# A hybrid block on one core: the queries and forget gates of heads 0 and 1 become a fourteenth seven-product unit, and their recurrence runs in the index stage

## The chip, the core and the metric

The kernel runs on one core of one Trainium2 chip. The core has a matrix engine (TensorE, PE in the profile, its weight loads PEld), a vector engine (VectorE, DVE), an activation engine (ScalarE, ACT), GpSimd (POOL) and SyncE (SP), which in this kernel issues nearly all transfers. Each engine works through its own instructions in order and waits on semaphores for the others. The metric is the device time of one execution in microseconds; the lower the better. The time before is 1340.77 us, the median of 3 runs (1340.67 to 1341.74).

## What is computed

One layer over 512 tokens of 2048 features, all in float32. The normalised input is projected by `w_in`; two branches follow, are each projected back to 2048 features, weighed by sigmoid gates, summed, projected once more, added to the input and normalised. The reference, cut to what matters:

```python
proj = rmsnorm(x, norm_w) @ w_in
a_q, a_f, a_i, a_g, c_q, c_kv, k_idx_raw, w_idx_raw, b_g, m_a, m_b = split(proj)
# branch A: gated linear recurrence, 8 heads of 128, chunks of 64 tokens
q = silu(a_q) * 128 ** -0.5
f = lb + (1 - lb) * sigmoid(a_f); k = 1 - f; log_f = log(f); v = a_i
y_a = rmsnorm(recurrence(q, k, log_f, v), gnorm_w) * silu(a_g)
# branch B: an indexer with 16 heads scores all keys, the best 128 a query are kept
score = sum_h relu(q_idx @ k_idx.T) * w_idx
y_b = softmax(q @ k_sel.T * 128 ** -0.5 + t5_bias) @ v_sel * silu(b_g)   # 8 heads of 128
merged = sigmoid(m_a) * (y_a @ w_pa) + sigmoid(m_b) * (y_b @ w_pb)
out = rmsnorm(x + merged @ w_out, final_norm_w)
```

The recurrence multiplies a state by the forget gate at each token, adds key times value, and reads it with the query.

## The kernel before

**Matmuls.** A float32 product is made of three matmuls on halves that carry a high and a low part (`mm3`, lines 74 to 77). The halves of the weights are made on the way: ScalarE writes `wh` (L71), VectorE subtracts to get `wl` (L72), from a raw tile `wr` that SP has loaded (L128). Two raw tiles exist; `load_ahead` keeps at most two loads beyond the splits, and `prep(i, ahead=3)` emits the splits up to two steps beyond the one in hand.

**Jobs.** The program is a list of jobs, emitted one after the other, which is also the order on every engine. `feat_job` projects `ntile` tiles of 128 features over `nk` blocks of the contraction, `kc` blocks to a step, with 512 tokens as columns. `pair_unit` computes 512 features at once by a scheme of seven products in place of eight: matrices are cut in quarters, VectorE and ScalarE make sums of quarters of the weights (`pair_sums`, L145 to L154), and each of 8 steps runs 7 products x 2 tiles x 3 matmuls of 256 columns. The gates of both branches go through eleven such units (`gate_pair`), and the queries and forget gates of head pairs 2 and 3 through two more (`pair_job` with `pair_evac` into `qf_d` in DRAM). Pairs 0 and 1 are projected by `af_aq(p)`: two `feat_job`s with two tiles and 16 blocks each.

**Lanes.** Work that isn't a large projection is written as generators in lanes (`hgrn` the recurrences, `top` the selection of keys, `att` attention, `norm`, `misc`, `t5`). `pump()` loads ahead, runs postponed stores (`flush`: a store asked for in `late` goes out two pumps later) and then takes one step of the first generator of each lane. `feat_job` pumps after each tile of a step when it has fewer than four tiles, else after each second one; with `often` also after block 1 of each tile. `drain(name)` runs a lane to its end at once.

**Recurrence** (`hgrn_gen(p)`, heads 2p and 2p+1). Seven levels: at odd levels TensorE computes scores into a bank `hl` (L80), VectorE multiplies by the decay (L784) and takes the scores over (L791, L797); at even levels ScalarE first copies (`keep`, L807), then VectorE multiplies again. Then keys are transposed (`hkt`), states (`hp`, `hst`) and outputs (`ho`) computed, normalised (`hz`), gated and stored to `ya_d` (L917). `R.load` tells the selection (`top_gen`) how much VectorE time a step takes; a round of the selection (two instructions over a block of scores, 48 rounds) is emitted when its credit, 2.7 less `R.load` at each pump, is above zero.

**Banks.** Eight PSUM banks: four `acc` for projections, four `sd`, handed out in turn, for the lanes and the indexer. An index head takes three `sd` banks for its scores `sc` (L75 to L77), which ScalarE empties by `relu` (L619).

**Order.** Start and first projections; pairs stage (thirteen units, 133 to 631 us); `open_branches`; index stage (eight `feat_job`s with `w_qidx`, 631 to 689 us), where the lane `hgrn` holds `early_gen()`, the forget gates of pairs 3 and 2; `end_index`, which opens the recurrences' pool and appends pairs 3 and 2; `ai_job(3)`, `ai_job(2)` (values); `af_aq(0)`, `af_aq(1)`, each of which appends its pair's recurrence at its end; `open_att`, which runs out norms, the T5 table and all but the last recurrence; `uqkv(0)` (attention's queries, keys and values of pair 0); `gate_job(44)`, the last four gate tiles, in eight steps, with callbacks that load `ya` and, after step 6, `end_hgrn`; `uqkv(1)`; then eight `w_pa` jobs with `uqkv(2)` and `uqkv(3)` behind the third and the fifth; eight `w_pb` jobs; the output projection.

**Attention** (`att_gen(p)`). `att_bias` loads a head's bias (`bh`, L967) and its gate and adds the selection's mask on GpSimd (`MB`, L971 to L974). Two pumps later `att_scores` runs the scores (`lA`, `lB`, `lC`) and their maxima; two pumps later come the exponentials (L1013) and the scaling (L1018); some pumps later `att_turn` transposes (`tA` to `tC`, L1029), and some later `att_values` multiplies by the values (`po`).

Of the kernel before, what the change touches and what calls it, by code (L numbers as in the profile page):

```python
# [50 lines left out]
def hybrid_block(ctx, tc, x, w_in, w_uq, w_qidx, w_ukv, w_pa, w_pb, w_out, rel_bias, final_norm_w,  # L51
# [51 lines left out]
    qf_d = dram.tile([2, 4, 128, T], F32, name="qf_d")  # L103
# [76 lines left out]
    lanes = {name: deque() for name in ("hgrn", "top", "att", "norm", "misc", "t5")}  # L180
# [14 lines left out]
    def pump():  # L195
# [19 lines left out]
    def feat_job(src, col, ntile, nk, kc, rhs, evac, before=None, width=T, after=None, place=0,  # L215
                 often=False):
# [5 lines left out]
        def run():  # L222
# [3 lines left out]
            for i in range(nk // kc):  # L226
                prep(at + i)
                wh, wl = halves.pop(at + i)
                for c in range(ntile):
                    for k in range(kc):  # L230
# [4 lines left out]
                        if often and k == 1:  # L235
                            pump()
# [3 lines left out]
                    if ntile < 4 or c % 2:  # L240
                        pump()
# [159 lines left out]
    def open_branches():  # L401
# [12 lines left out]
        R.i = enter("norms")  # L414
        R.ckv = R.i.tile([128, 2, T], F32, name="ckv")
        SP.dma_start(R.ckv, ckv_d.rearrange("f p t -> p f t"))
        early_load(3)
        lanes["hgrn"].append(early_gen())

    def t5_gen():  # L420
        rb = R.i.tile([128, H], F32, name="rb")
        rbs = [R.i.tile([128, H], FR, name=f"rb{i}") for i in "hl"]
        oh = R.i.tile([128, 384], FR, name="oh")
        tl = R.i.tile([H, 384], F32, name="tl")
        ts = [R.i.tile([H, 384], FR, name=f"tl{i}", tag=f"sum{i}") for i in "hl"]
        flip = R.i.tile([128, 128], FR, name="flip")
        far = R.i.tile([H, 1], F32, name="far")
        G.memset(rb, 0.0)
        SP.dma_start(rb[0:32], rel_bias)
        raw = R.i.tile([128, 512], F32, name="nt", bufs=2)  # L430
# [19 lines left out]
        for h in range(0, H, 2):  # L450
            bf = R.i.tile([128, 2, 2, 256], FR, name="bf")
# [9 lines left out]
            e = R.i.tile([128, 2, 256], F32, name="nt", bufs=2)  # L461
# [4 lines left out]
    def lb_gen():  # L466
        mx = R.i.tile([128, H], F32, name="mx")
# [27 lines left out]
    def rstd_row(ps, width, r=None):  # L495
        r = R.i.tile([128, T], F32, name="rr") if r is None else r
        A.activation(r, ps, AF.Ln, bias=eps, scale=1.0 / width)
        A.activation(r, r, AF.Exp, scale=-0.5)
        return r

    def q_sums(j0):

        for j in (j0, j0 + 1):
            s = R.i.tile([128, T], F32, name="nsq", bufs=2)
            A.activation(s, R.cq[:, j, :], AF.Square)
            if j == 0:
                R.qs = R.i.tile([128, T], F32, name="qs")
# [8 lines left out]
        sh = R.i.tile([128, T], FR, name="sumh")  # L516
        sl = R.i.tile([128, T], FR, name="suml")
# [26 lines left out]
    def norm_gen(raw, n, w, hi, lo):  # L544
        ss = []
        for j in range(n):
            ss.append(R.i.tile([128, T], F32, name="nsq", bufs=2))
# [4 lines left out]
        sh = R.i.tile([128, T], FR, name="sumh")  # L552
# [166 lines left out]
    def early_gen():  # L719
        for p in (3, 2):  # L720
            for _ in range(4):
                yield
# [908 lines left out]
```

## Time and profile before

| | |
|---|---|
| median of 3 runs | 1340.77 us |
| span of the profiled execution, first to last instruction | 1338.4 us |
| transfers over the span | 205.82 MB, mean 154 GB/s |
| index stage, first `sc` to the last | 636.9 to 689.3 us |
| levels of pairs 3, 2, 0, 1 begin (first `hl`) | 695.1, 754.9, 813.7, 866.3 us |
| first `w_pa` matmul | 945.1 us |
| last attention transposition begins | 1071.2 us |

The page lists busy time for each engine, the span in 40 slices, the DMA queues, the chain that ended last, and the costliest groups of instructions. A window's row has the stretch, its length, then for PE, PEld, DVE, ACT and POOL the busy time and in brackets the number of instructions, then the granted TensorE clock as a share, the DMA engines' share and GB/s. A row of the waits says which engine, tile and line waited for which, then the total, the number of waits and the longest. A row of the timeline has the start, the duration, engine, line, operation, output and inputs, shapes, count, and in square brackets idle time before it with what ended it. Matmuls are pipelined: one is shown longer than the distance to the next start.

The program takes 2.4 us more in the runs than the profiled span shows from its first to its last instruction.

### The profile page before, as it was taken

Reading aid. Unit: us, or ns where it says so; the run is one execution under the profiler, and the core shown is the slowest. Engines: PE = TensorE matmul, PEld = TensorE weight load, DVE = VectorE, ACT = ScalarE, POOL = GpSimd, SP = SyncE. Lnnn points to the kernel's source line nnn. Section 1 sums busy time; section 2 is a strip of 40 time slices with the busy share of each in tenths; the row PEclk is TensorE's granted clock in tenths of the full one; section 3 lists DMA queues with packets and bytes.
Section 4 is the critical chain, followed back from the end, with each engine's and each line's share of the span. In section 5 each row is a group of like instructions: output and inputs, shape, how many; then the busy total and the mean of one; then the engine's idle time right before and its main releaser. Section 6 shows DMA issues by size and latency. Waiting matters only on the chain.

```text
span 1338.4 us, 26561 instructions
## 1 busy us (share of the span) xinstructions
PE 1327.9 (99%) x10876; PEld 1236.6 (92%) x10876; DVE 1068.6 (80%) x1705; ACT 666.8 (50%) x1060; POOL 39.0 (3%) x54
## 2 busy tenths in 40 slices
PE   9999999999999999999999999999999999999997
PEld 8988999999999999999999888888888888899996
DVE  7777889998888888886778988875656658899856
ACT  6455555454454444443666465656434423444435
POOL 2000000000000000000000000020001000000000
PEclk9999999999999999999999999999999999999999
DMA  6343545543454444434523525445655556653454
GB/s 243 93 112 113 155 142 158 148 141 107 143 158 143 142 143 142 128 113 159 181 85 110 182 73 158 127 149 178 242 193 189 186 177 220 201 162 123 168 202 166
DMA packets 141290, 205.82 MB, mean 154 GB/s; under 512 B 8672, under 2 KB 82032, under 8 KB 141040
## 3 DMA queue, kind: packets, MB, share of 16 engines
q1 hardware_dynamic: 140592, 203.78, 48.3%
q8 instruction: 85, 1.39, 0.4%
q10 hardware_dynamic: 576, 0.35, 0.1%
q14 instruction: 37, 0.30, 0.1%
HBM read 168.42 MB, written 35.68 MB: 152 GB/s over the span
## 4 chain that ended last, share of the span: by engine, by line
PE 96%; DMA 1%; DVE 1%; ACT 1%; SPq 0%; issue 0%; ACTq 0%; DVEq 0%
PE pp L75 15%; PE pp L77 15%; PE pp L76 15%; PE acc L75 14%; PE acc L76 14%; PE acc L77 14%; PE hl L80 1%; PE ho L80 1%; DMA wr<-in_w_in_dram 1%; PE sc L75 1%; PE sc L76 1%; PE sc L77 1%; DMA xt<-in_x_t_dram 0%; PE hp L80 0%; PE po L77 0%; PE po L76 0%
## 5 line engine op out<-in xcount | busy, mean ns | idle before, releaser
L150 ACT ACTIVATE bh<-wr 128x768 fp32r<-128x768 f32 x128 | 108.2, 845 | 215.3 <-issue 99.7
L152 ACT ACTIVATE wh<-sv 128x512 fp32r<-128x512 f32 x256 | 152.3, 623 | 84.4 <-DVE sv L145 66.9
L75 PE MATMUL pp<-sh,wh 128*128 128x256 f32 x624 | 172.7, 277 | 0.0
L77 PE MATMUL pp<-sh,wl 128*128 128x256 f32 x624 | 172.7, 277 | 0.0
L76 PE MATMUL pp<-sl,wh 128*128 128x256 f32 x624 | 172.6, 277 | 0.0
L72 DVE TENSOR_TENSOR wl<-wr,wh 128x1024 fp32r<-128x1024 f32 (+1 forms) x104 | 125.6, 1209 | 56.7 <-ACT wh L71 56.7
L154 DVE TENSOR_TENSOR wl<-sv,wh 128x1024 fp32r<-128x1024 f32 x128 | 156.5, 1222 | 6.1
L153 DVE TENSOR_TENSOR bl<-wr,bh 128x768 fp32r<-128x768 f32 x128 | 122.2, 955 | 46.9 <-ACT bh L150 46.2
L71 ACT ACTIVATE wh<-wr 128x1024 fp32r<-128x1024 f32 (+1 forms) x104 | 108.2, 1040 | 92.2 <-PE acc L76 44.1
L75 PE MATMUL acc<-xh,wh 128*128 128x512 f32 x304 | 120.3, 396 | 0.0
L76 PE MATMUL acc<-xl,wh 128*128 128x512 f32 x304 | 118.5, 390 | 0.0
L77 PE MATMUL acc<-xh,wl 128*128 128x512 f32 x304 | 118.5, 390 | 0.0
L76 PEld LDWEIGHTS pp<-sl,wh 128*128 128x128 f32 x624 | 117.3, 188 | 0.0
L75 PEld LDWEIGHTS pp<-sh,wh 128*128 128x128 f32 x624 | 117.3, 188 | 0.0
L77 PEld LDWEIGHTS pp<-sh,wl 128*128 128x128 f32 x624 | 117.3, 188 | 0.0
L75 PE MATMUL pp<-xh,bh 128*128 128x256 f32 x416 | 114.8, 276 | 0.0
L77 PE MATMUL pp<-xh,bl 128*128 128x256 f32 x416 | 114.8, 276 | 0.0
L76 PE MATMUL pp<-xl,bh 128*128 128x256 f32 x416 | 114.8, 276 | 0.0
L75 PE MATMUL acc<-yh,wh 128*128 128x512 f32 x256 | 100.3, 392 | 0.0
L76 PE MATMUL acc<-yl,wh 128*128 128x512 f32 x256 | 99.7, 390 | 0.0
L77 PE MATMUL acc<-yh,wl 128*128 128x512 f32 x256 | 99.7, 389 | 0.0
L145 DVE TENSOR_TENSOR sv<-wr 128x512 f32<-128x512 f32 x128 | 87.9, 686 | 7.2 <-DMA wr<-in_w_in_dram 4.4
(390 smaller groups left out, 3608.4 us busy)
## 6 DMA issues: line engine op xcount, KB each, us to landing
wr<-in_w_in_dram SPq DMA_DIRECT2D x136, 512.0 KB, 3.8
wr<-in_w_out_dram SPq DMA_DIRECT2D x32, 512.0 KB, 3.8
mg<-gate_d SPq DMA_DIRECT2D x48, 256.0 KB, 4.2
gate_d<-c SPq DMA_DIRECT2D x44, 256.0 KB, 4.9
wr<-in_w_in_dram SPq DMA_DIRECT2D x36, 256.0 KB, 3.0
wr<-in_w_pa_dram SPq DMA_DIRECT2D x16, 512.0 KB, 4.3
wr<-in_w_pb_dram SPq DMA_DIRECT2D x16, 512.0 KB, 4.1
wr<-in_w_qidx_dram SPq DMA_DIRECT2D x8, 512.0 KB, 4.1
```

The costliest lines, as they stand in the source:

```text
L71: A.activation(hi, src, AF.Copy)
L72: V.tensor_tensor(lo, src, hi.bitcast(F32), op=OP.subtract)
L75: PE.matmul(ps, lh, rh, start=first, stop=False, skip_group_check=True)
L76: PE.matmul(ps, lh, rl, start=False, stop=False, skip_group_check=True)
L77: PE.matmul(ps, ll, rh, start=False, stop=last, skip_group_check=True)
L80: PE.matmul(ps, l, r, start=first, stop=last, skip_group_check=True)
L145: V.tensor_tensor(sv[:, 0:2, :], b[:, 1:3, :], b[:, 0:1, :].to_broadcast([128, 2, 256]), op=OP.add)
L150: A.activation(bh, b[:, 1:4, :], AF.Copy)
L152: A.activation(vh[:, i:i + 2, :], sv[:, i:i + 2, :], AF.Copy)
L153: V.tensor_tensor(bl, b[:, 1:4, :], bh.bitcast(F32), op=OP.subtract)
L154: V.tensor_tensor(vl, sv, vh.bitcast(F32), op=OP.subtract)
```

## The change

The queries and forget gates of pair 0 are computed in the pairs stage as a fourteenth unit, ahead of those of pairs 2 and 3; `qf_d` grows from four to six head slots, and `early` says where each pair lies. `af_aq(0)` goes. The recurrences' pool opens before the index stage; pair 0's forget gates and recurrence stand first in the lane `hgrn`, pair 3's and pair 2's forget gates are in a lane of their own, `early`. `uqkv(0)` moves behind `gate_job(44)`, and `uqkv(1)` to `uqkv(3)` behind the second, fourth and sixth `w_pa` job; `open_att` goes, and `end_hgrn` runs out recurrences, norms and the T5 table. `ukv_job` first runs out the selection. `gate_job(44)` pumps after each tile in its steps 3 to 6; in `w_pa` jobs `often` means three extra pumps a step in place of two, and the selection's credit at a pump is told by the caller (`room`). Most tiles of the norms move to a pool `R.n`.

```diff
-    qf_d = dram.tile([2, 4, 128, T], F32, name="qf_d")
+    qf_d = dram.tile([2, 6, 128, T], F32, name="qf_d")
+    early = {0: 0, 2: 2, 3: 4}
...
-    lanes = {name: deque() for name in ("hgrn", "top", "att", "norm", "misc", "t5")}
+    lanes = {name: deque() for name in ("hgrn", "top", "att", "early", "norm", "misc", "t5")}
...
-    def pump():
+    def pump(room=2.7):
+        R.room = room
...
-                        if often and k == 1:
-                            pump()
+                        if often and (c, k) in ((0, 1), (1, 0), (1, 2)):
+                            pump(0.75)
...
-                    if ntile < 4 or c % 2:
-                        pump()
+                    if ntile < 4 or c % 2 or i in fine:
+                        pump(0.75 if often else 1.36 if i in fine else 2.7)
...
-        R.i = enter("norms")
+        R.h = enter("hgrn")
+        R.i = enter("parts")
         R.ckv = R.i.tile([128, 2, T], F32, name="ckv")
+        early_load(0)
+        early_load(3)
         SP.dma_start(R.ckv, ckv_d.rearrange("f p t -> p f t"))
-        early_load(3)
-        lanes["hgrn"].append(early_gen())
+        lanes["hgrn"].extend((early_gen(0), hgrn_gen(0)))
+        lanes["early"].append(early_gen(3))
...
-                    credit += 2.7 - R.load
+                    credit += R.room - R.load
...
-    def early_gen():
-        for p in (3, 2):
-            for _ in range(4):
+    def early_gen(p):
+        if p == 2:
+            for _ in range(3):
                 yield
-            for c in range(2):
-                forget(p, c)
-                yield
-            if p == 3:
-                early_load(2)
+            early_load(p)
+        for _ in range(3):
+            yield
+        for c in range(2):
+            forget(p, c)
+            yield
...
+        if p == 0:
+            lanes["early"].append(early_gen(2))
         yield
...
         def run():
+            drain("top")
             drain("att")
...
-        feat_job(w_in, GATE_COL[j0], 4, NK, 2, x_rhs, evac, after=after)
+        feat_job(w_in, GATE_COL[j0], 4, NK, 2, x_rhs, evac, after=after, fine=range(3, 7))
...
-        for p in (2, 3) if j == 16 else ():
+        for p in early if j == 16 else ():
...
-        R.h = enter("hgrn", side="right")
+        R.n = enter("extra", side="right")
...
-    af_aq(0)
+    af_aq(1)
     jobs.append(lambda: load_v(1))
-    af_aq(1)
-    jobs.append(open_att)
-    uqkv(0)
...
     def end_hgrn():
-        drain("hgrn")
+        for name in ("hgrn", "norm", "t5"):
+            drain(name)
         flush()
         flush()
+        leave("parts")
         leave("hgrn")
+        leave("extra")
         R.u = enter("us", side="right")
+        R.a = enter("att")
         load_y(R.ya, ya_d, 2, 4)
...
-                  3: lambda: (take_x(R.ya, 1), load_y(R.ya, ya_d, 4, 8)),
+                  4: lambda: (take_x(R.ya, 1), load_y(R.ya, ya_d, 4, 8)),
...
-    uqkv(1)
-    jobs.append(lambda: load_y(R.yb, yb_d, 0, 2))
+    uqkv(0)
...
-        if j in (4, 8):
+        if j in (2, 6, 10):
             uqkv(j // 4 + 1)
-        if j in (6, 10):
-            jobs.append(lambda h=j // 2 - 1: load_y(R.yb, yb_d, h, h + 2))
+        if j in (4, 8, 12):
+            jobs.append(lambda h=j // 2 - 2: load_y(R.yb, yb_d, h, h + 2))
```

More of the change, by code (lines that the diff above doesn't have):

```diff
@@ L215, in feat_job @@
     def feat_job(src, col, ntile, nk, kc, rhs, evac, before=None, width=T, after=None, place=0,
-                 often=False):
+                 often=False, fine=()):
         at = len(specs)
@@ L413, in open_branches @@
         G.tensor_copy(R.levels, lev)
-        R.i = enter("norms")
+        R.h = enter("hgrn")
+        R.i = enter("parts")
         R.ckv = R.i.tile([128, 2, T], F32, name="ckv")
+        early_load(0)
+        early_load(3)
         SP.dma_start(R.ckv, ckv_d.rearrange("f p t -> p f t"))
-        early_load(3)
-        lanes["hgrn"].append(early_gen())
+        lanes["hgrn"].extend((early_gen(0), hgrn_gen(0)))
+        lanes["early"].append(early_gen(3))
     def t5_gen():
[L421 to L427, printed above, removed]
+        rb = R.n.tile([128, H], F32, name="rb")
+        rbs = [R.n.tile([128, H], FR, name=f"rb{i}") for i in "hl"]
+        oh = R.n.tile([128, 384], FR, name="oh")
+        tl = R.n.tile([H, 384], F32, name="tl")
+        ts = [R.n.tile([H, 384], FR, name=f"tl{i}", tag=f"sum{i}") for i in "hl"]
+        flip = R.n.tile([128, 128], FR, name="flip")
+        far = R.n.tile([H, 1], F32, name="far")
         G.memset(rb, 0.0)
         SP.dma_start(rb[0:32], rel_bias)
-        raw = R.i.tile([128, 512], F32, name="nt", bufs=2)
+        raw = R.n.tile([128, 512], F32, name="nt", bufs=2)
         SP.dma_start(raw[:, 0:384], c_buckets)
@@ L503, in q_sums @@
         for j in (j0, j0 + 1):
[L504 removed]
+            s = R.n.tile([128, T], F32, name="nsq", bufs=2)
             A.activation(s, R.cq[:, j, :], AF.Square)
             if j == 0:
[L507 removed]
+                R.qs = R.n.tile([128, T], F32, name="qs")
                 first = s
@@ L515, in q_sums @@
             return
-        sh = R.i.tile([128, T], FR, name="sumh")
-        sl = R.i.tile([128, T], FR, name="suml")
+        sh = R.n.tile([128, T], FR, name="sumh")
+        sl = R.n.tile([128, T], FR, name="suml")
         split(sh, sl, R.qs)
@@ L551, in norm_gen @@
         yield
-        sh = R.i.tile([128, T], FR, name="sumh")
-        sl = R.i.tile([128, T], FR, name="suml")
+        sh = R.n.tile([128, T], FR, name="sumh")
+        sl = R.n.tile([128, T], FR, name="suml")
         split(sh, sl, ss[-1])
@@ L650, in place @@
     def place(p, shape, dtype, name, tag):
-        if p == 1 or tag not in ("hf", "hq"):
+        if tag not in ("hf", "hq"):
             return R.h.tile(shape, dtype, name=name, tag=tag)
-        return R.i.tile(shape, dtype, name=name, tag=f"{tag}{p or 3}")
+        return R.i.tile(shape, dtype, name=name, tag=f"{tag}{p % 2}")
     def load_v(p):
@@ L716, in early_load @@
             hg[p, n] = place(p, [128, 2, T], F32, "h" + n, "h" + n)
-            SP.dma_start(hg[p, n], qf_d[i, 2 * p - 4:2 * p - 2].rearrange("f p t -> p f t"))
-    def early_gen():
-        for p in (3, 2):
-            for _ in range(4):
+            SP.dma_start(hg[p, n], qf_d[i, early[p]:early[p] + 2].rearrange("f p t -> p f t"))
+    def early_gen(p):
+        if p == 2:
+            for _ in range(3):
                 yield
-            for c in range(2):
-                forget(p, c)
-                yield
-            if p == 3:
-                early_load(2)
+            early_load(p)
[4 more added lines that the diff above has]
+            yield
     def aq_evac(p):
@@ L1089, in open_norms @@
         R.rq = R.r.tile([128, T], F32, name="rq")
-        R.i = enter("norms", side="right")
+        R.i = R.n = enter("norms", side="right")
         R.cq = R.i.tile([128, 4, T], F32, name="cq")
@@ L1224, in hybrid_block @@
             lane("norm", q_rows)
-        for p in (2, 3) if j == 16 else ():
+        for p in early if j == 16 else ():
             pair_job(w_in, [p * 256, 1024 + p * 256], NK // 2, x_pair,
-                     pair_evac([qf_d[i, 2 * p - 4:2 * p - 2] for i in range(2)], [AF.Silu, AF.Sigmoid]))
+                     pair_evac([qf_d[i, early[p]:early[p] + 2] for i in range(2)], [AF.Silu, AF.Sigmoid]))
         gate_pair(j)
@@ L1250, in end_index @@
         lanes["t5"].append(t5_gen())
-    def open_att():
-        drain("norm")
-        drain("t5")
-        while len(lanes["hgrn"]) > 1:
-            for _ in lanes["hgrn"].popleft():
-                pass
-        flush()
-        flush()
-        leave("norms")
-        R.a = enter("att")
     def af_aq(p):
```

12 lines of the change are left out of this document (6 added, 6 removed).

## The prediction

> **What bounds the kernel now.** I read the page first, then the waits of TensorE, then windows, then the timeline where the change cuts.
>
> ```profile
> span 1338.4 us, 26561 instructions
> PE 1327.9 (99%) x10876; PEld 1236.6 (92%) x10876; DVE 1068.6 (80%) x1705; ACT 666.8 (50%) x1060; POOL 39.0 (3%) x54
> PE acc L310 <- POOL ones_r L306: 1.4, 1, 1.4
> PE pf L80 <- ACT xh L340: 0.6, 1, 0.6
> PE pf L80 <- POOL fh L336: 0.3, 1, 0.3
> PE pf L80 <- DVE fl L342: 0.3, 1, 0.3
> ```
>
> The last four rows are the whole list of TensorE's waits: 2.6 us, all in the start-up. TensorE is the bound from end to end, so every column of matmul saved is time saved, and every wait that the change gives TensorE is time lost, since no later slack takes it back. The question is the balance of the two.
>
> **The saving.** The two jobs of `af_aq(0)` go: 2 x 16 x 2 x 3 = 192 matmuls of 512 columns. One unit of seven products comes: 8 x 7 x 2 x 3 = 336 matmuls of 256 columns.
>
> ```profile
> 210.00:248.24 38.24, 38.24 (x339) 38.24 (x338) 35.62 (x52) 19.19 (x32) 0.00 (x0) 1.00 0.50 152
> ...
> 964.91 0.45 PE L75 MATMUL lA<-ak,aq 128*128 128x512 f32 x1
> 966.77 0.40 PE L75 MATMUL acc<-yh,wh 128*128 128x512 f32 x1
> 974.97 0.60 PE L1029 MATMUL tA<-ident,P 128*128 128x128 f32 x4
> ```
>
> The first row is a window cut to one unit (span, then busy time and count of PE, PEld, DVE, ACT, POOL): 38.24 us for 336 matmuls (three at its edges belong to the neighbours), 0.1138 us each. Between 966.77 and 974.97 lie 36 matmuls of 512 columns: 8.20 / 36 = 0.228 us. Removed 192 x 0.228 = 43.7 us, added 38.2 us: **minus 5.5 us**. VectorE is busy 35.6 of the unit's 38.2 us, so preparing the pairs hides under the matmuls, as in the thirteen units that run; without that cover at most a unit's evictions, some 5 us, would show. The unit's loads and stores are those of its neighbours.
>
> [...]
>
> **What the change moves.** A "pump" hands out one step of each lane. I count them from the code. The index stage has 16, `ai_job(3)` and `ai_job(2)` 8 each, `af_aq(1)` 16: 48 before `gate_job(44)`. Its steps 0 to 2 have 2 each, 2.73 us of matmuls apart, steps 3 to 6 have 4 each, 6 x 0.228 = 1.36 us apart. The lane of the recurrences needs 5 (forget gates of pair 0), 17 (pair 0), 16 (pair 3), 17 (pair 2) and 18 (pair 1). So pair 0 starts at pump 6, in the index stage, and pair 1 at pump 56: its level steps 1 to 7 fall on pumps 58 to 64, all of them 1.36 us apart, where the kernel before gave it 2.73. Three of its steps are left to `end_hgrn`; they hold no matmul.
>
> *The fine pumps.* An odd level's matmuls (L80 `hl`) need the even level's decay, which needs a ScalarE copy, which needs the odd decay:
>
> ```profile
> 813.71 0.73 PE L80 MATMUL hl<-hq,hqk 128*32 128x32 f32 x62
> 815.05 1.23 DVE L784 TENSOR_TENSOR hqk<-hqk,hf 128x1024 f32<-128x1024 f32 x1 [0.81 <-PE hl L80]
> 817.52 1.25 DVE L72 TENSOR_TENSOR wl<-wr,wh 128x1024 fp32r<-128x1024 f32 x1
> 818.70 1.21 DVE L784 TENSOR_TENSOR hqk<-hqk,tot 128x1024 f32<-128x1024 f32 x1
> 820.61 0.71 PE L80 MATMUL hl<-hq 128*32 128x16 f32 x62
> 821.93 1.23 DVE L784 TENSOR_TENSOR hqk<-hqk,tot 128x1024 f32<-128x1024 f32 x1 [0.30 <-PE hl L80]
> 823.25 1.07 ACT L807 ACTIVATE hq<-hqk 128x1024 f32<-128x1024 f32 x1 [1.70 <-DVE hqk L784]
> 825.09 1.22 DVE L784 TENSOR_TENSOR hqk<-hqk,tot 128x1024 f32<-128x1024 f32 x1
> 827.50 0.70 PE L80 MATMUL hl<-hq 128*32 128x16 f32 x62
> ```
>
> From level 1's first matmul to the end of level 2's decay it is 819.91 - 813.71 = 6.2 us with a weight split (`wl`) in between, 5.1 without; from level 3 to 4, 826.31 - 820.61 = 5.7 and 5.0; I take 5.5 and 4.9 for 5 to 6. Today odd levels lie 6.9 us apart (813.71, 820.61, 827.50), so nothing shows. On fine pumps they would lie 2 x 1.36 + 1.3 for the level's own matmuls = 4.1 us apart. One split comes per four pumps, and by the count the pumps 58 to 60 and 62 to 64 hold one each: TensorE waits 2.1 + 1.0 + 1.4 = **4.5 us**. Bounds: 0 if the levels fell on wide pumps, 5.5 with a split in all three and a wait at the norm.
>
> *The start of the index stage.* `early_load(0)` puts two more loads of 512 KB on SP's queue ahead of `ckv` and of the next index weights.
>
> ```profile
> 636.38 0.51 SPq L416 DMA_DIRECT2D ckv<-ckv_d  x1
> 636.93 0.47 SPq L717 DMA_DIRECT2D hq<-qf_d  x1
> 637.45 0.47 SPq L717 DMA_DIRECT2D hf<-qf_d  x1
> 638.01 15.57 SPq L128 DMA_DIRECT2D wr<-in_w_qidx_dram  x4
> ...
> 638.00:642.00 4.00, 4.00 (x25) 3.87 (x24) 2.97 (x6) 2.12 (x6) 1.85 (x4) 1.00 0.98 335
> 640.00:642.00 2.00, 2.00 (x13) 1.87 (x12) 0.97 (x3) 1.05 (x3) 1.32 (x3) 1.00 1.04 398
> ...
> 645.48 1.06 ACT L71 ACTIVATE wh<-wr 128x1024 fp32r<-128x1024 f32 x1 [2.73 <-DMA wr<-in_w_qidx_dram]
> 646.44 0.47 ACT L71 ACTIVATE qih<-acc 128x384 fp32r<-128x384 f32 x1
> 646.81 0.81 ACT L712 ACTIVATE hf<-hf,lb,oml 128x512 f32<-128x512 f32 x1
> 647.52 1.24 ACT L619 ACTIVATE relu<-sc 128x512 f32<-128x512 f32 x3
> ...
> 648.59 0.34 PE L75 MATMUL sc<-kih,qih 128*128 128x384 f32 x1
> ```
>
> The DMA engines are full there (share 0.98, 335 GB/s), and ScalarE already stands 2.73 us for those weights, with the `relu` that empties a score bank queued behind. That bank is taken again by the second block of the next head, at 648.59; its `relu` ends at about 648.1, half a microsecond ahead. One more MB takes 1.05 / 0.34 = 3.1 us, 2.6 at the 0.40 MB/us of its fastest stretch, and a second forget gate adds 0.7 on ScalarE: 2.6 + 0.7 - 0.5, about **3 us** of wait. Bounds 0 (nothing moves if the loads are issued earlier than I think) and 5 (3.1 + 1.4 for two gates + 0.5). Behind it pair 0's levels and values to pump 16 bring VectorE some 16 us in a stage where it now has this:
>
> ```profile
> 637.00:691.00 54.00, 54.00 (x315) 51.82 (x314) 42.18 (x72) 36.37 (x75) 1.85 (x4) 1.00 0.41 131
> ```
>
> That is 58 us in 54 + 6.6 (the recurrence's matmuls): nearly full, odd levels 8.7 us apart against a chain of 6; I cost it at 0.
>
> *From `gate_job(44)` to the first `w_pa` job.* Before, attention of pair 0 filled this place; now 5.5 + 5.5 + 5.5 = 16.4 us lie between `end_hgrn` (step 6) and `w_pa`, and a chain of transfers runs in it:
>
> ```profile
> 926.00 2.66 SPq L917 DMA_DIRECT2D ya_d<-hy  x4
> 931.16 0.37 SPq L1285 DMA_DIRECT2D yh<-ya_d  x1
> 932.25 0.42 SPq L128 DMA_DIRECT2D wr<-in_w_pa_dram  x1
> ...
> 867.19 0.47 SPq L967 DMA_DIRECT2D bh<-bh_d  x1
> ...
> 872.01 0.46 POOL L971 TENSOR_TENSOR MB<-M,bh 128x128 f32<-128x128 f32 x1 [33.40 <-DMA bh<-bh_d]
> 872.43 4.28 POOL L974 TENSOR_TENSOR MB<-M,bh 128x256 f32<-128x256 f32 x3
> ```
>
> SP stands at the load of `ya_d` until the stores have landed (5.2 us from 926.00 to 931.16). Queued behind it are the second weights of `w_pa`, and behind their split, on ScalarE, the split of attention's keys, whose banks `w_pa` takes next. Norm and split (4.6 us), stores 5.2, load and weights about 6: some 16 us after step 6, just when `w_pa` starts. `bh` comes later still; its mask additions end 9.5 us after its issue here (867.19 to 876.7), while scores now follow two pumps (2.7 us) behind, and the transposition six more. I take **1.5 us**, bounds 0 and 5 (two waits of 2.5). The new `drain("top")` has the keys' matmuls and the splits behind it; by the credits the selection is one round short or done there, so 0.
>
> *Attention at finer pumps.* From the scores to the transposition lie six pumps. For a second head they hold 36 matmuls, and VectorE's last scaling of the probabilities ends just ahead:
>
> ```profile
> 972.57 1.27 DVE L1018 TENSOR_SCALAR P<-P,sm 128x512 f32<-128x512 f32 x4
> ```
>
> It ends at 973.84, the transposition starts at 974.97: slack 1.1 us. The new pattern (6, 6, 3, 6, 3 matmuls) gives 27 or 30 in six pumps, 1.4 to 2.1 us less: 0.3 to 1.0 us late, on four such heads; first heads have about twice the slack. **2 us**, bounds 0 and 4 (eight heads at 0.5).
>
> **Sum**: -5.5 + 4.5 + 3.0 + 1.5 + 2.0 = +5.5 us. The span of 1338.4 becomes 1343.9; the median of the runs, 1340.77, lies 2.4 us above that span (what is around it, taken as unchanged): **1346.3 us**.
>
> **The rivals.** (a) *Everything hides*: the waits list is empty today, and queues and banks have absorbed all this so far; then 1340.8 - 5.5 = 1335.3. This is the other side, slower turned faster, and it is decided in the fine pumps: once the odd levels of pair 1 come under 4.1 us apart, or fall on wide pumps, the gain stays. Against it speaks the chain of 5 us, which is dependence and not load. With one or two small waits up to 1338.1 it is still faster: 15%. (b) *It cancels*: the levels cost their 4.5, the rest nearly nothing: 1340 to 1343, centre 1341; 27%. (c) *It takes longer than I say*: each place at its upper bound gives -5.5 + 5.5 + 5 + 5 + 4 = +14, 1354.8; 10%, half of it above 1352. (d) *The unit doesn't save*: spacing of 256-column matmuls worse per column; the rows exclude it. My forecast, 1343.5 to 1349 with its middle at 1346.3, has 48%.
>
> Each of my waits is under 3 us. [...]
>
> Differences under 0.2%, 2.7 us, can't be told from none here. Faster (under 1338.1) 0.15, same 0.27, slower (over 1343.5) 0.58. The range is 1337 to 1352: it takes in most of (b), some of (a), and leaves the ends of (a) and (c) out.
>
> **What would show it.** Right: TensorE's waits list gets rows `hl` from DVE `hqk` (three of 1 to 2 us in `gate_job(44)`), `sc` from ACT `relu` in the first third of the index stage, `acc` from ACT or DVE near the first `w_pa` job, `tA` from DVE `P`; the matmuls' own sum falls by 5.5 us. Wrong: the levels of pair 1 are 4.1 us apart without a wait, or lie outside steps 3 to 6; ScalarE's wait for index weights doesn't grow beyond 2.73 us; the transpositions keep a slack.

## The result and the profile after

The changed kernel takes 1356.31 us (median of 4 runs, 1354.23 to 1357.83) against 1340.72 us: ratio 1.0117, interval 1.0102 to 1.0131. It is slower by 15.6 us where 5.5 had been forecast, and outside the range. The profiled execution took 1357.11 us, its span is 1355.3 (1.8 us less, where the sum had taken 2.4). First the head of its page.

```profile
span 1355.3 us, 26958 instructions
PE 1332.4 (98%) x11020; PEld 1243.9 (92%) x11020; DVE 1090.2 (80%) x1744; ACT 670.8 (49%) x1074; POOL 35.6 (3%) x54
```

Then the list of TensorE's waits.

```profile
PE hl L80 <- DVE hqk L790: 2.2, 3, 0.9
PE sc L75 <- ACT relu L624: 2.1, 2, 1.1
PE acc L75 <- ACT gs L1207: 2.1, 1, 2.1
PE hl L80 <- ACT hqk L756: 2.0, 1, 2.0
PE tA L1038 <- DVE P L1027: 2.0, 3, 1.4
PE acc L312 <- POOL ones_r L308: 1.4, 1, 1.4
PE hl L80 <- issue: 0.8, 1, 0.8
PE t L80 <- DVE rbl L72: 0.8, 1, 0.8
PE hl L80 <- DVE hqk L757: 0.7, 1, 0.7
```

Before, the list held 2.6 us, all in the start-up. Now some 12 us of new waits stand in five places. `hl` after VectorE's `hqk` in the gate job (two of the three waits of L790), `sc` after `relu` and `tA` after `P` are rows that the prediction named. `hl` after ScalarE's `hqk` (L756) is not, and the `hl` waits in the `ai` jobs (L757 and the third of L790) aren't either. `acc` after `gs` has the form of a row that was named, but it waits for another bank than the one described there.

A fuller account needs more than this list, for it leaves out a slower clock and small gaps. I took from both traces, for each matmul, the distance to the next one's start, and subtracted the median distance of its form. What is left, summed by stage, is TensorE's lost time:

| stage | lost before | lost after | more | forecast |
|---|---|---|---|---|
| start and pairs stage | 9.1 | 10.4 | 1.2 | 0 |
| index stage | 0.7 | 5.8 | 5.1 | 3.0 |
| `ai` jobs | 2.4 | 5.1 | 2.8 | 0 |
| `af_aq` jobs (two before, one after) | 4.4 | 2.3 | -2.1 | 0 |
| `gate_job(44)`, steps 0 to 6 | 1.8 | 9.0 | 7.3 | 4.5 |
| its step 7, and `uqkv` up to the first `w_pa` | 0.3 | 4.2 | 3.9 | 1.5 |
| `w_pa` jobs | 1.6 | 5.9 | 4.4 | 2.0 |
| `w_pb`, output | 1.9 | 2.0 | 0.1 | 0 |

The medians themselves sum to 1306.6 us before and 1300.9 after: the unit saved 5.7. So -5.7 + 22.6 = +16.9, the difference of the spans. The start varies by as much between kernels that have it in common (9.0 lost in e3, 10.4 here), so its 1.2 need not be the change's. Index and `af_aq` belong together (a recurrence moved from the one to the other): +3.0.

Where pair 1's first level stands late, the timeline after (VectorE, ScalarE, TensorE) shows what is ahead of it:

```profile
876.68 0.69 DVE L649 MAX8 m<-M 128x8 f32<-128x512 f32 x1
...
879.21 0.69 DVE L649 MAX8 m<-M 128x8 f32<-128x512 f32 x1
...
880.60 1.22 DVE L72 TENSOR_TENSOR wl<-wr,wh 128x1024 fp32r<-128x1024 f32 x1
881.73 1.29 DVE L72 TENSOR_TENSOR hy<-hqk,hy 128x512 fp32r<-128x512 f32 x2
...
883.05 1.06 ACT L756 ACTIVATE hqk<-hf 128x1024 f32<-128x1024 f32 x1 [2.57 <-DVE hy L72]
...
884.16 0.94 PE L80 MATMUL hl<-hq,hqk 128*32 128x32 f32 x63 [1.99 <-ACT hqk L756]
```

Read it upwards: TensorE waits for a ScalarE copy, this for VectorE's split `hy` of the pair before, and VectorE did two rounds of the selection and a weight split first. Next, the instructions of the selection's line, before (L644) and after (L649), in the groups by line:

```profile
L644 DVE MAX8 m<-M x48: 420/556/695, 702.2 to 848.7; 128x8 f32<-128x256 f32 x16, 128x8 f32<-128x384 f32 x16, 128x8 f32<-128x512 f32 x16
```

```profile
L649 DVE MAX8 m<-M x48: 408/554/695, 749.3 to 933.0; 128x8 f32<-128x256 f32 x16, 128x8 f32<-128x384 f32 x16, 128x8 f32<-128x512 f32 x16
```

The same 48 rounds begin 47 us later and end 84 us later, 4.2 us ahead of the first `w_pa` matmul (937.2); before, they ended 96 us ahead of it (945.1). Windows of that line alone tell under which jobs they run (VectorE's busy time and, in brackets, the rounds). Before, the `ai` jobs and the two `af_aq` jobs; after, the `ai` jobs, the one `af_aq` job, `gate_job(44)`, and what lies between its last matmul and `w_pa`:

```profile
689.40:746.60 57.20, 7.90 (x18) 1.00 0.37 105
746.60:858.00 111.40, 18.85 (x30) 1.00 0.42 131
```

```profile
739.20:799.80 60.60, 7.29 (x17) 1.00 0.46 139
799.80:855.00 55.20, 10.38 (x18) 1.00 0.49 145
855.00:921.90 66.90, 6.21 (x9) 0.97 0.40 132
921.90:937.20 15.30, 2.75 (x4) 0.89 0.80 274
```

The windows after, of all engines, show VectorE over that time, and two short stretches of TensorE:

```profile
755.00:845.00 90.00, 87.73 (x1322) 78.81 (x1322) 80.46 (x162) 45.04 (x64) 2.23 (x3) 1.00 0.52 158
...
879.00:916.00 37.00, 32.66 (x565) 26.97 (x565) 22.83 (x37) 17.20 (x30) 0.96 (x1) 0.95 0.48 158
916.00:937.00 21.00, 18.91 (x87) 15.55 (x86) 17.16 (x29) 13.33 (x19) 0.00 (x0) 0.92 0.58 201
...
884.50:887.90 3.40, 3.40 (x117) 2.98 (x103) 1.87 (x3) 1.16 (x2) 0.00 (x0) 0.50 0.94 297
925.40:928.80 3.40, 3.40 (x9) 2.65 (x9) 2.40 (x4) 1.36 (x2) 0.00 (x0) 0.50 0.89 278
```

VectorE (the third pair) is 89% busy from 755 to 845, then only 62% in pair 1's zone from 879 to 916, where behind the round at 879.2 none follows until 916.1: the credit of 1.36 a fine pump is below the levels' load. The last two rows have a granted clock of 0.50, 3.4 us each, behind the two longest waits (881.8 to 884.2, 921.9 to 924.4). They cost 2.7 us together: the matmuls lie 0.43 us apart there in place of 0.228.

### The profile page after: what moved, and what is told of

It is laid out like the page before. It is cut to its first block, busy times and chain, and to the rows that moved or that the text cites. A ratio compares the mean times of both kernels' runs of the same rounds, so it can differ in the third digit from the quotient of the medians.

```text
span 1355.3 us, 26958 instructions
## 1 busy us (share of the span) xinstructions
PE 1332.4 (98%) x11020; PEld 1243.9 (92%) x11020; DVE 1090.2 (80%) x1744; ACT 670.8 (49%) x1074; POOL 35.6 (3%) x54
## 3 DMA queue, kind: packets, MB, share of 16 engines
q8 instruction: 86, 1.41, 0.4%
## 4 chain that ended last, share of the span: by engine, by line
PE 88%; DVE 6%; ACT 3%; DMA 2%; issue 1%; POOL 0%; SPq 0%; DVEq 0%; ACTq 0%
PE pp L76 16%; PE pp L75 16%; PE pp L77 16%; PE acc L75 11%; PE acc L76 10%; PE acc L77 10%; PE pf L80 2%; PE hl L80 1%; DVE wl L72 1%; PE ho L80 1%; DVE hqk L790 1%; DMA wr<-in_w_qidx_dram 1%; DVE M L650 1%; PE sc L75 1%; DVE m L649 0%
## 5 line engine op out<-in xcount | busy, mean ns | idle before, releaser
L153 ACT ACTIVATE wh<-sv 128x512 fp32r<-128x512 f32 x272 | 162.0, 624 | 89.5 <-DVE sv L146 71.1
L77 PE MATMUL pp<-sh,wl 128*128 128x256 f32 x672 | 186.1, 277 | 0.0
L75 PE MATMUL pp<-sh,wh 128*128 128x256 f32 x672 | 186.0, 277 | 0.0
L76 PE MATMUL pp<-sl,wh 128*128 128x256 f32 x672 | 186.0, 277 | 0.0
L155 DVE TENSOR_TENSOR wl<-sv,wh 128x1024 fp32r<-128x1024 f32 x136 | 166.2, 1222 | 6.6 <-ACT wh L153 0.3
L72 DVE TENSOR_TENSOR wl<-wr,wh 128x1024 fp32r<-128x1024 f32 (+1 forms) x96 | 115.5, 1204 | 47.9 <-ACT wh L71 47.9
L76 PEld LDWEIGHTS pp<-sl,wh 128*128 128x128 f32 x672 | 126.4, 188 | 0.0
L75 PE MATMUL acc<-xh,wh 128*128 128x512 f32 x240 | 95.7, 399 | 0.0
L77 PE MATMUL acc<-xh,wl 128*128 128x512 f32 x240 | 93.9, 391 | 0.0
L76 PE MATMUL acc<-xl,wh 128*128 128x512 f32 x240 | 93.8, 391 | 0.0
```

Source lines behind the costliest of these rows:

```text
L72: V.tensor_tensor(lo, src, hi.bitcast(F32), op=OP.subtract)
L75: PE.matmul(ps, lh, rh, start=first, stop=False, skip_group_check=True)
L76: PE.matmul(ps, lh, rl, start=False, stop=False, skip_group_check=True)
L77: PE.matmul(ps, ll, rh, start=False, stop=last, skip_group_check=True)
L153: A.activation(vh[:, i:i + 2, :], sv[:, i:i + 2, :], AF.Copy)
L155: V.tensor_tensor(vl, sv, vh.bitcast(F32), op=OP.subtract)
```

## The experiments

The theory at first was a row of separate waits: remove one and its length comes back. The rival was that chains stand side by side, so that the next one takes over.

**The loads of pair 3 and `ckv` three pumps later (e1).**

```diff
-        early_load(3)
-        SP.dma_start(R.ckv, ckv_d.rearrange("f p t -> p f t"))
...
-        if p == 2:
+        if p:
             for _ in range(3):
                 yield
             early_load(p)
+        if p == 3:
+            SP.dma_start(R.ckv, ckv_d.rearrange("f p t -> p f t"))
```

> The loads of pair 3's queries and forget gates and of the key/value ranks are issued some pumps later, behind the first index weights. If the two waits of the index scores for a relu (1.3 and 1.2 us in the changed kernel) come from the loads queued ahead of the weights, both go and the time falls by 2.5 us, to about 1354. Rival: VectorE has too much work in the shortened stages as a whole, so a wait taken away in one place comes back in another and the time stays at 1356.

1352.51 us, ratio 1.0086 (1.0071 to 1.0101): 3.8 us less than the change. Both `relu` waits are gone, and the index stage loses 3.1 us in place of 5.8, which is 2.7 of the 3.8. The loads were the cause, and the term of 3.0 was right in size. The profile has no stretch at half the clock, where the change's has two, so the clock may have a part in the rest.

**Fine pumps from step 1 (e2).**

```diff
-        feat_job(w_in, GATE_COL[j0], 4, NK, 2, x_rhs, evac, after=after, fine=range(3, 7))
+        feat_job(w_in, GATE_COL[j0], 4, NK, 2, x_rhs, evac, after=after, fine=range(1, 7))
```

> gate_job(44) pumps after each tile from step 1 on, not from step 3, so that the last recurrence has ended by the end of step 6 and nothing is left to end_hgrn. If the wait of the first uq matmul for a bank (2.25 us, and 1.6 us of half clock behind it) comes from that tail on ScalarE, it goes: about 3.9 us less, 1352.5. The waits at the levels, about 5 us with the half clock there, stay. Rival (VectorE too full as a whole): no change, 1356.

1356.3 us, 1.0114 (1.0098 to 1.0129): no gain, as the rival had it. The wait for `gs` fell from 2.25 to 0.34 us, so it did come from the recurrence's tail; in its place a wait for the split of attention's keys (`ak`) came at the first `w_pa` matmul (list of waits of this run):

```profile
PE acc L75 <- DVE ak L72: 4.0, 1, 4.0
PE hl L80 <- DVE hqk L790: 3.1, 3, 1.4
```

**Pump points of `gate_job(44)` set apart (e3).** Every six matmuls in general, nine at pair 1's levels.

```diff
+                        if points and k < kc - 1 and (i * ntile + c) * kc + k + 1 in points:
+                            pump(1.6)
...
-                    if ntile < 4 or c % 2 or i in fine:
+                    if points:
+                        if (i * ntile + c + 1) * kc in points:
+                            pump(1.6)
+                    elif ntile < 4 or c % 2 or i in fine:
...
-        feat_job(w_in, GATE_COL[j0], 4, NK, 2, x_rhs, evac, after=after, fine=range(3, 7))
+        feat_job(w_in, GATE_COL[j0], 4, NK, 2, x_rhs, evac, after=after, points=(*range(2, 19, 2), *range(21, 40, 3), *range(40, 57, 2), 60, 64))
```

> gate_job(44) pumps after every 6 matmuls, but after every 9 at the seven levels of the last recurrence, and is done with it by step 6. Levels then lie 2.05 us of matmuls apart: by the chain of the levels some 1 us of waits is left of 3.2, the wait at its first level (2.15 us) and its half clock shrink, and the tail at uq goes as with e2: 6 to 9 us less, 1347 to 1350. Rival (VectorE too full as a whole): no change, 1356. If only the tail counts: as e2.

1355.16 us, 1.0109 (1.0092 to 1.0126). The waits at the levels behind the first went: their chain at fine pumps was the cause, as forecast. But the first level's wait stayed (2.0 us), and the wait for `ak` stood here too, 4.0 us, with a stretch at half the clock, and took the gain.

**Unread matmuls where TensorE would wait (e4).** Eight ahead of pair 1's first level and nine ahead of `uqkv(0)`, into a bank that nobody reads, to see whether the clock then stays whole.

```diff
+    def heat(n):
+        ps = bank("heat")
+        for _ in range(n):
+            PE.matmul(ps, ones_r, R.ckh[:, 0, :], start=True, stop=True, skip_group_check=True)
```

> The changed kernel with 8 matmuls of 512 columns that nobody reads ahead of level 1 of pair 1, and 9 ahead of the first uq matmul: 17 x 0.228 = 3.9 us of work put into two waits of 2.15 and 2.25 us. If it is the idle time that halves the clock afterwards (two stretches of 3.4 us in the trace), the clock stays whole and the time falls by up to 3 us, to about 1353.5, though work is added. Rival: the low clock comes from elsewhere or costs nothing, then the time stays at 1356, or rises by what doesn't fit into the waits.

1356.27 us, 1.011 (1.0095 to 1.0125). The clock was whole at both places, but it fell elsewhere, for 6.8 us, behind the first of two level waits of 1.5 and 1.2 us. The price of the clock is not settled by this run.

**A second buffer for `hqk` (e5), norms and T5 seven pumps later (e6), the load of `y` behind step 7 on top of e2 (e7).**

```diff
-        qk = R.h.tile([128, 2, 2, T], F32, name="hqk")
+        qk = R.h.tile([128, 2, 2, T], F32, name="hqk", bufs=2)
...
     def norm_gen(raw, n, w, hi, lo):
+        for _ in range(7):
+            yield
...
-        load_y(R.ya, ya_d, 2, 4)
...
-                  6: end_hgrn, 7: lambda: take_x(R.yb, 2)})
+                  6: end_hgrn, 7: lambda: (take_x(R.yb, 2), load_y(R.ya, ya_d, 2, 4))})
```

> The changed kernel with two buffers for the recurrence's query/key tile (hqk) in place of one. In the changed kernel TensorE waits 2.0 us at the first level of pair 1 for ScalarE's copy into that tile, and ScalarE had waited for VectorE to have split the last outputs of pair 2 out of it. If the one buffer is the cause, that wait goes, with the half clock it brings in some executions: 2 to 3.5 us less, 1353 to 1354.5. Rival: VectorE is behind there with selection rounds, the multiplication into the tile comes late as well, and the wait stays: 1356.

> The changed kernel with the norm of the key/value ranks and the T5 table begun 7 pumps later, so that they meet the levels of pair 3, where the selection holds back, as they did before the change. If the two waits at pair 3's levels (0.9 and 1.0 us) come from these two and the selection together ahead of the levels, they go: 2 to 3 us less, about 1354. Rival: VectorE is full over the whole stretch, the work has to be done somewhere, and the waits move to other levels: 1356.

> The run with pumps after each tile from step 1 on (1356.3), in which a wait of 4.0 us for the split of attention's keys had taken the place of the one for a gate bank; here the load of heads 2 and 3 of ya is issued behind step 7, so that the second weights of w_pa no longer stand behind it on SP's queue. If that order is the cause, the 4.0 us and the 1.6 us of half clock go: about 1351. Rival: the split of the keys is late because ScalarE and VectorE have too much ahead of it: 1355 to 1356.

1355.33 (1.011, 1.0095 to 1.0125), 1354.48 (1.0101, 1.0086 to 1.0117) and 1355.29 us (1.0107, 1.0092 to 1.0122). None of the three is clear of the change, whose runs reach from 1354.23 to 1357.83, so what they show is in their waits. In e5 the ScalarE copy no longer waits, and VectorE's product for the same level (L757) is late in its place (2.5 us in two waits, 0.7 in one in the change), which is the rival. In e6 the two waits in the `ai` jobs fell from 0.88 and 0.98 to 0.30 and 0.51. In e7 the `ak` wait stayed (4.0 us), so SP's queue is not what makes it. VectorE's timeline of e7 shows what does:

```profile
929.41 0.70 DVE L649 MAX8 m<-M 128x8 f32<-128x512 f32 x1
...
930.93 0.69 DVE L649 MAX8 m<-M 128x8 f32<-128x512 f32 x1
...
932.45 0.43 DVE L652 TENSOR_SCALAR M<-M 128x512 f32<-128x512 f32 x1
932.79 1.22 DVE L72 TENSOR_TENSOR wl<-wr,wh 128x1024 fp32r<-128x1024 f32 x1
933.93 1.28 DVE L72 TENSOR_TENSOR ak<-acc,ak 128x512 fp32r<-128x512 f32 x2
```

The last rounds, run out by `drain("top")`, stand directly ahead of the weight split and of the split that empties the keys' bank. Six rounds begin behind the last gate matmul there, five in e3, four in the change.

**All of these together (e8):** loads, norms, second buffer, points, the load of `y`, and one more pump ahead of attention's turns of pairs 0 to 2; attention of pair 0 also begins one pump earlier, with its scores one pump later behind the mask.

> The changed kernel with all repairs at once: loads later, norms and T5 table later, two buffers, levels 9 matmuls apart, ya load behind step 7, attention of pair 0 begun one pump earlier with its scores one pump later after the mask, and one more pump ahead of the transpositions of pairs 0 to 2. If the loss is the sum of separate waits, the parts add: -2.5 -2 -2.2 -2 -3.9 -3 and some 2 of half clock, 1338 to 1341, level with the kernel before. Rival (VectorE too full as a whole): most of it comes back elsewhere, 1350 or more.

1351.65 us, 1.0087 (1.007 to 1.0103), as the rival had it. Index and `ai` are better, but the longest wait of its list, and 6.8 us at half the clock around it, remain:

```profile
PE acc L75 <- DVE ak L72: 3.9, 1, 3.9
```

So the selection became the suspect. **Half of its rounds (24), in the changed kernel (e9) and in the one before (e10)**. The mask is then another one: these kernels leave out half of the selection and serve to measure only.

```diff
-            for i in range(16):
+            for i in range(8):
...
-                if i == 15:
+                if i == 7:
```

> The changed kernel with 8 rounds of the selection for each block of rows in place of 16 (24 rounds in place of 48; the mask is then another one, everything else stays). The trace of the changed kernel has its last round at 933.0 us, 4 rounds behind the last gate matmul (921.5) and two directly ahead of pair 1's first level (876.7 and 879.2); the kernel before had its last at 848.7. Theory, the selection that came 47 us later fills VectorE where pair 1 and attention's keys need it: the wait of 2.15 us ahead of pair 1's first level goes, so do most of the 2.25 us for uq's bank and the half-clock stretches behind both (1.1 to 1.6 each), 4 to 7 us in all: 1349 to 1352. Rival, ScalarE's own row (hy, weight halves, sigmoid) sets these waits: they stay within 0.5 us, 1354 to 1357.

> The kernel before with the same 24 rounds in place of 48, as a control. Theory: its selection ended 22 us ahead of the gate job and nothing waited behind it, so 1340 to 1341, ratio 0.999 to 1.001. Rival, VectorE was full there too and half the rounds make any kernel faster: 1336 to 1338.5.

e10: 1340.73 us, 1.0001 (0.9991 to 1.001). Before, the rounds cost nothing, though VectorE spends 25 us on 24 of them (1090.2 busy in the changed kernel, 1065.4 in e9). e9: 1355.05 us, 1.0107 (1.0092 to 1.0122), only 1.3 less than the change; the theory fell in this form. Its waits:

```profile
PE hl L80 <- DVE hqk L790: 2.2, 2, 1.4
PE acc L75 <- ACT gs L1207: 2.1, 1, 2.1
```

The first level's wait is gone. But the level behind it waits 1.5 us in place of 0.6, a level in the `ai` jobs 1.9 in place of 0.9, and `gs`, a sigmoid behind other work of ScalarE, is where it was; the profile has three stretches at half the clock in place of two. So this run doesn't price the rounds by themselves.

**All 48 rounds earlier (e11), and with e1, e5 and e6 (e12).** The edit gives 3.6 of credit where the caller of a pump names none. While rounds are handed out, that is in the `ai` jobs alone, since `feat_job` names its own 2.7: 27 rounds now run under the `ai` jobs in place of 17, and 17 in place of 18 under the `af_aq` job.

```diff
-    def pump(room=2.7):
+    def pump(room=3.6):
```

> The changed kernel whole, with 3.6 us of VectorE credit at an ordinary pump in place of 2.7: the same 48 rounds, all of them emitted ahead of the fine pumps. Theory, only the place of the rounds matters: what half the rounds gain is nearly all gained here, less some 1 us of new waits in the ai jobs, where VectorE is busy for 13.7 to 14.7 of 15 us: 1350 to 1353, last round before 880. Rival, the rounds push VectorE's splits and pair 3's levels back where it is full: excess in ai from 5.1 to over 8 us and 1355 to 1358.

> The earlier selection together with the loads 3 pumps later, the norms and T5 7 pumps later and the second buffer of hqk; pump points and the y load as in the change. Theory, the repairs were held back by the selection's rounds: minus 3.8 for the loads, minus 1 to 2 for the norms, minus 4 to 5 for the selection: 1345 to 1348. Rival, each freed wait is taken by the next chain, as in the kernel with all repairs (1351.65): 1350 to 1353.

1360.7 us (1.0148, 1.0131 to 1.0165) and 1356.9 us (1.0123, 1.0108 to 1.0139): e11 by the rival's mechanism, both longer than even the rivals had it. The rounds now end at 870.8 in e11, but the `ai` jobs, where VectorE was full, lose 10.4 us in place of 5.1. Under the `ai` jobs the rounds can't be had for nothing.

**e3 and e9 in one (e13).**

> The kernel with pair 1's levels apart and 8 selection rounds for each block of rows in place of 16 (another mask). Theory, two limits stand one behind the other: the levels' own chain, which the later pump points relieve, and behind it the selection rounds that must be done ahead of attention's keys (5 of them behind the last gate matmul in that kernel, keys' bank 4.1 us late and half clock behind it). With both taken away the 4.1 us and the 1.6 us behind it go: 1349 to 1351. Rival, the keys' bank is late for another reason (the loads of y and of w_pa): its wait stays above 3 us and the time is 1354 to 1356.

1348.49 us, 1.0058 (1.0042 to 1.0075), a little better than expected. Alone e3 gains 1.2 and e9 1.3, neither clear of the scatter; together they gain 7.8. Two limits lie one behind the other, and each hid the other. `gate_job(44)` with step 7 and `uqkv` loses 5.2 us in place of 13.2, and both the `ak` and the `gs` rows are out of the list.

**e8 with all rounds, 3.6 of credit at the pumps of the `af_aq` job (e14), and that with attention's pumps and the load of `y` as in the change (e15).** The first gate steps, which the expectation names too, keep their 1.6: in e8 the gate job pumps at its own points.

```diff
-                        pump(0.75 if often else 1.36 if i in fine else 2.7)
+                        pump(0.75 if often else 1.36 if i in fine else 3.6)
```

> The kernel with all repairs (1351.65) whole, with more VectorE credit (3.6 us) at the pumps of af, aq and the first gate steps only, behind the ai jobs: all rounds emitted ahead of pair 1's first level. Theory, what is left there is the drain of 5 rounds ahead of the keys: 4.1 us of wait and 3.1 us from half the clock go, 1 to 2 us of new waits in af and aq: 1346 to 1348. Rival, the waits move to the levels, as when the rounds came earlier everywhere (1360.7): 1350 to 1354.

> As the kernel with repairs and earlier selection, but attention's pumps and the load of y as in the change. Theory: attention's first turns are a chain of their own, 1.5 to 2.3 us late in nearly every run; with its pumps as they were the w_pa stage loses within 1 us of the other form: 1346 to 1349. Rival, the added turns brought 2 to 3 us of waits there (7.2 us lost in that stage, 5.9 in the changed kernel): 1344 to 1345.5.

1352.02 us (1.0087, 1.0072 to 1.0102) and 1355.2 us (1.0106, 1.0091 to 1.0122): by its time the rival in e14, though at the levels of the `af_aq` job and not at pair 1's; and neither in e15. In e14 everything from the gate job to `w_pa` is nearly clean (4.5 us lost), but the `af_aq` job loses 11.7 us in place of 2.3:

```profile
PE hl L80 <- DVE hqk L766: 2.6, 2, 2.4
PE t L80 <- DMA bf<-t_d: 2.3, 2, 1.5
```

In e15 `w_pa` loses 6.2 us against 5.5 in e14: the spacing of attention's turns is worth under 1 us. Most of the rest of the difference between the two profiles is a stop of TensorE of 2.8 us in the `ai` jobs and half the clock behind it (last section).

**e8 with half the rounds (e16), and e8 with all rounds put among pair 1's levels, 2.0 of credit in place of 1.6 at the gate job's pumps (e17).**

> The kernel with all repairs (1351.65) with 8 selection rounds for each block of rows in place of 16 (another mask). Theory, the repairs of the index stage and of the norms add to 1348.5 once the selection's rounds are out of the way, since these waits lie in other places: minus 3 for the loads, minus 1.5 to 2.5 for the ai jobs: 1343 to 1345. What is then left above 1335 would be attention's turns and the start of ai. Rival, the waits go on moving: 1347 to 1350.

> The kernel with all repairs whole, with 2.0 us of VectorE credit in place of 1.6 at the pumps of the gate job: none of the rounds is left for the drain ahead of the keys; two more stand ahead of pair 1's first levels and six ahead of its tail. Theory, VectorE has room among the levels (10.1 of 17 us busy there in the changed kernel), so the 4.1 us wait and the half clock behind it go for 1 to 2 us of level waits: 1347 to 1349. Rival, each round among the levels lengthens their chain by its 1.5 us: 1351 to 1354.

e16: 1342.46 us, 1.0015 (1.0005 to 1.0024). e17: 1348.85 us, 1.0063 (1.0047 to 1.008). Both as the theory had it, e16 even below its range. The waits of e16, then those of e17:

```profile
PE tA L1050 <- DVE P L1039: 2.8, 5, 0.8
PE acc L317 <- POOL ones_r L313: 1.4, 1, 1.4
PE pf L80 <- POOL fh L343: 0.8, 1, 0.8
PE hp L80 <- ACT hkd L873: 0.6, 1, 0.6
```

```profile
PE acc L77 <- issue: 2.2, 1, 2.2
PE tA L1050 <- DVE P L1039: 1.8, 5, 0.4
PE hl L80 <- DVE hqk L766: 1.6, 1, 1.6
PE hl L80 <- ACT hqk L765: 1.6, 1, 1.6
```

With half the rounds nothing is left but attention's transpositions and small waits, and the clock is whole throughout; the keys' wait is gone with the rounds. What still keeps e16 from a gain is the `w_pa` stage: it loses 4.9 us more than in the kernel before, against the 5.7 that the unit saves. With all of the rounds, the best complete form of the change has two waits of 1.6 at pair 1's first levels, and 3.4 us at half the clock behind. It is 7.5 us faster than the change and still 8.6 slower than the kernel before (1340.28 in that set of runs). No complete form that I ran beats that one.

## Why the prediction was wrong

**Right in direction, and in what a wait costs.** TensorE was the bound, and the waits given to it were lost. The saving was 5.7 us for a forecast of 5.5; the matmul spacing of the trace held (0.228 us at 512 columns, 0.114 at 256).

**The index stage** was sized right: 3.0 forecast, 3.0 found with the recurrence's move taken out, 3.8 by e1. Its waits, `sc` after `relu`, are the row that was named, and stand where it was named, in the first third. The zero for VectorE behind them ("nearly full ... I cost it at 0") held: with the loads moved (e1), the index stage and the `af_aq` job together lose under half a microsecond more than before.

**The fine pumps**: the level waits behind the first were smaller than the 4.5 forecast (0.64 + 0.22, 0.32 + 0.97 and 1.09: 3.2 us), and e3 shows that the spacing makes them. What was missed is the wait ahead of the chain: pair 1's first level stood 2.15 us for VectorE, and some 1.1 us of the half clock fell behind it. The stage lost 7.3.

**The step that failed** is the overlap that was taken for granted: the sum prices four places and puts nothing on what VectorE and ScalarE have to do between them. For the selection it says so: for `drain("top")` "by the credits the selection is one round short or done there, so 0". The count was made at that one place. Over the whole stretch it comes out otherwise: the 48 rounds start at 749 in place of 702, because the fourteenth unit and pair 0's recurrence are now ahead of them, and of the two projections under which the last 30 used to run, `af_aq(0)` is gone. So 13 rounds are left for the gate job and what follows. Two of them stand directly ahead of pair 1's first level; with half the rounds (e9) its wait goes. Four come behind the last gate matmul. In the change they cost the keys nothing, but with five or six there (e2, e3, e7, e8) the keys' bank is some 4 us late. In the repaired kernel half of the rounds are worth 9.2 us (e8 to e16); before, nothing (e10).

The rounds don't explain the change by themselves: with the change's own pump points, half of them gave 1.3 (e9). The loss is a set of chains on VectorE and ScalarE, side by side between the index stage and attention's keys. The sum worked out each place alone, as if what stands ahead of it on its engine were on time. By the table it was short by 2.8 us in the `ai` jobs, 2.8 in the gate job, 2.4 in `uqkv(0)` and 2.4 in the `w_pa` jobs, and right in the index stage.

**From the gate job to `w_pa`** the forecast was 1.5 and the loss 3.9, with other causes. The chain of `ya`, its store and SP, that I described, is not what TensorE met. The profile after has on ScalarE, in order, `hy`, a weight half, a table load, and then the sigmoid that frees `uqkv(0)`'s bank:

```profile
920.34 1.15 ACT L71 ACTIVATE hy<-hqk 128x512 fp32r<-128x512 f32 x2 [1.29 <-DVE hqk L916]
921.40 1.04 ACT L71 ACTIVATE wh<-wr 128x1024 fp32r<-128x1024 f32 x1
922.46 1.28 ACT L1207 ACT_TABLE_LOAD   x1
923.75 2.07 ACT L1207 ACTIVATE gs<-acc 128x512 f32<-128x512 f32 x4
```

That wait is 2.25 us, and 1.6 more is the clock at half behind it. With the recurrence's tail done earlier (e2) it is 0.34. e7 shows that the place of `y`'s load does not matter where the rounds are in the way.

**The `ai` jobs** were not in the sum and lost 2.8: pair 3's levels stand behind selection, norm and T5 on VectorE. e6 (2.8 to 1.5) and e16 (0.6) show it.

**Attention's turns**: forecast 2.0, lost 4.4, with the named row. The 2.0 was low by its own terms: four heads at 0.3 to 1.0 us are 1.2 to 4.0, 2.6 in the middle. And the first turn of all was 1.57 us late, one of the "first heads" that I had given twice the slack. The sum took VectorE's scaling of the probabilities at the 1.27 us of the row shown. Ahead of that turn it took longer, while GpSimd was adding the next head's mask:

```profile
946.71 2.30 POOL L983 TENSOR_TENSOR MB<-M,bh 128x256 f32<-128x256 f32 x3
947.54 2.14 DVE L1027 TENSOR_SCALAR P<-P,sm 128x512 f32<-128x512 f32 x4
```

In the change the other late turn has 1.97 us ahead of it, and the four late ones of e16, which still loses 6.5 us in this stage, have 2.27 to 2.94, each with GpSimd at work; without it the scaling takes 1.27 us in both. Before, it was drawn out twice too (1.58 and 2.01 us), with more slack behind. No run set the two apart, so how much of the stage's loss this is stays open.

**The clock** had no term in the sum, where each wait was to be "under 3 us". Here waits of 2.15 and 2.25 us were each followed by half the clock (0.50 for 3.4 us), 2.7 us in all.

**The rivals.** That of upper bounds (1354.8) came nearest in time, but not by its places. That on the other side, where everything hides, has its condition met in e3 and e13: pair 1's later levels come without a wait, yet 1355.2 and 1348.5 are not 1335.3. The fine pumps alone did not decide. *It cancels* (1341) had the levels at their cost and the rest at nearly nothing; the rest was the larger part. That the unit doesn't save is out: it saved 5.7.

## What to carry to other kernels

When a projection is removed, ask what was done under it: list all work with a deadline on each helping engine between the place that starts it and the place that needs it, and compare its length with TensorE's time there, over the whole stretch and not at single points. Waits that stand one behind another can't be priced or tested one at a time: two edits worth 1.2 and 1.3 us alone were worth 7.8 together. Before believing that work can be moved, find a stretch where its engine is idle and nothing in the chain stands behind it; the windows showed it (62% against 89%), and rounds put there (e17) were worth 2.8 us over e8.

## What the runs showed of the hardware

The granted clock fell to 0.50 for 3.4 us (twice for 6.8) at TensorE waits. Over all profiles, with waits measured by the spacing of the matmuls, such a stretch began at each of nine waits from 2.5 to 4.1 us, four times before its end and at the latest 1.6 us after it, and no later than 3.4 us after 14 of 38 waits from 1.5 to 2.4 us. The two stretches that are left stand at waits of 2.7 and 2.2 us in the lists of e11 and e12 (`t` for `rbl`). The kernel before, e10 and e16, with no wait above 1.2 us behind the start-up, had none. From 1.5 to 2.4 us the length alone doesn't tell: the same wait for `gs`, 2.25 us, had a stretch behind it in the change, e5 and e9, and none in e1, e6, e11 and e12. What decides it isn't shown.

TensorE also stopped at the same matmul of the `ai` jobs without a releaser, 0.16 us in e14, 0.7 in e8, 2.2 in e17 and 2.8 in e15, where this window lies wholly in it:

```profile
766.00:768.00 2.00, 0.00 (x0) 0.00 (x0) 2.00 (x4) 0.76 (x2) 0.00 (x0) 1.00 1.02 388
```

The DMA engines are full then (share 1.02, 388 GB/s), and nearly so in the other three (0.95 and more). That alone is not enough: in e16 they are as full (1.04 from 764 to 766 us), and TensorE goes on. The traces have a nearer lead. The DMA queue q8 carries packets of 16 KB of the kind `instruction`, 86 in the profile after (1.41 MB); an estimate from that is 64 bytes for each of TensorE's 22040 matmuls and weight loads, so I take them for its instructions. The packet nearest to the stop had come at 762.6 us in e16, without a stop; at 763.9 in e14, 765.4 in e8, 766.6 in e17 and 766.9 in e15, and TensorE went on 0.5 us (e8) to 1.3 us behind it. So my estimate from these times is that the instructions came late through the full DMA engines; no run moved them, so it isn't shown.
